# A convolution's sums on GpSimd, fewer weight tiles used whole, and the layer norm placed behind the convolution

## The chip, the cores and the metric

The kernel runs on 1 core of one Trainium2 chip. The metric is the device time of one execution in microseconds. One core has TensorE (PE, with its weight loads as PEld), VectorE (DVE), ScalarE (ACT), GpSimd (POOL) and SyncE (SP), each with its own queue, in which instructions are taken in program order; between engines they wait on semaphores.

## What is computed

Two blocks over 256 positions of 1024 channels, in float32. The first block has two layers, each a gated feed-forward, a mixer with short convolutions and a state-space part, a second feed-forward and a gated projection. The change lies in the second block, in its mixer:

```python
def conformer_conv(glu_in, conv_w, conv_b, ln_g, ln_b, w_conv_out):
    a, gate = jnp.split(glu_in, 2, axis=-1)
    v = a * jax.nn.sigmoid(gate)
    rhs = conv_w.astype(v.dtype)[:, None, :]
    v = lax.conv_general_dilated(v, rhs, window_strides=(1,), padding=[(CONV_K - 1, 0)],
                                 dimension_numbers=('NWC', 'WIO', 'NWC'),
                                 feature_group_count=CONV_WIDTH) + conv_b
    v = layernorm(v, ln_g, ln_b)
    v = jax.nn.silu(v)
    return v @ w_conv_out
...
h = rmsnorm_2(x, norm_mix_pre[l])
proj = h @ w_in[l]
u_pool, u_glu, g_a, g_b = jnp.split(proj, ...)
branch_a = pool_mixer(u_pool, pool_w[l], pool_scale[l], w_pool_out[l])
branch_b = conformer_conv(u_glu, conv_w[l], conv_b[l], conv_ln_g[l], conv_ln_b[l], w_conv_out[l])
merged = jax.nn.sigmoid(g_a) * branch_a + jax.nn.sigmoid(g_b) * branch_b
x = x + rmsnorm_2(merged @ w_o[l], norm_mix_post[l])
```

The convolution is causal and goes channel by channel, with 31 taps over 512 channels. The pool branch takes trailing means of 512 channels, a small product per group, and a projection. A feed-forward with a squared ReLU follows.

## The kernel before

Channels lie on the 128 partitions, the 256 positions along the free dimension. All weights lie in one stream of 4948 tiles of 128x128 in the order of their use. They come in pieces of 8 tiles through four buffers (`raw`). For most pieces ACT rounds the piece into `whi` (line 324) and DVE takes the difference into `wlo` (line 327), through a ring of five pairs; activations are split the same way (`split`, line 401). A tile then is three matmuls: hi by hi, hi by lo, lo by hi (line 366). The pieces between `WHOLE[0]` and `WHOLE[1]` are left as they are, and their tiles are multiplied in full float32 with an operand that isn't split (`Whole`, line 1369; `mm3`, line 375); the trace shows such a tile as two records. Here these are the last 104 tiles of `w_in_2`: 13 of the second block's 16 gate units.

A unit is 128 output channels: it takes a PSUM bank and multiplies its tiles, and a small routine then works off the bank. The order of instructions on each engine is made at build time by a small planner (`Flow`): routines run as generators, each operation adds an estimated cost to its engine's clock, and whichever routine is due next issues next. So the text of the program sets the order only in part; the costs set the rest.

The second block (`second`, line 978) first makes `xf`, the normed input that isn't split, and then works through `w_in_2` in this order: four pairs of units for the gated linear unit (`glu_part`), four for the pool branch (`pooled`), 16 for the two gates (`gate`), the first `NSPLIT` = 3 of them with split weights. A gate on split weights is multiplied by the norm's row on DVE first; one on whole weights is not, since `xf` has the row in it. Beside these units runs the convolution. The accumulator `cacc` (4 groups of 128 channels) starts with tap 30 and the bias on ACT (`conv_start`). For the other 30 taps there are two ways: ACT scales the shifted input into one of three product buffers (`conv_products`, ring `pr`) and DVE adds that product, 128x1024, to `cacc`; or DVE does a fused multiply-add for each of the four groups (`conv_sums`). `conv_sums` adds a product when one is ready and otherwise takes a tap from the other end.

When all units of `w_in_2` are issued, `layer_norm` is started: it waits for the sum (`cvdone`), takes a column sum on TensorE with a matrix of ones, subtracts the mean, squares, takes a second column sum, and makes the norm's row; `ln_out` then gives the four operands of `w_conv_out_2`. Beside it TensorE does `pool_w_2` (4 tiles) and `w_pool_out_2` (32 tiles); `w_conv_out_2` (32 tiles) follows.

In the profile `x` is the tile whose parts are `xf`, `cacc` and the product buffers, `sga` the gates, `cv` and `vv` scratch of the pool branch. Lines 237, 244, 257 and 266 are those of the helpers for a matmul, a two-operand DVE instruction, a fused DVE instruction and an activation.

Of the kernel before, what the change touches and what calls it, by code (L numbers as in the profile page):

```python
# [17 lines left out]
P = 128  # L18
T = 256
D = 1024  # L20
ND = D // P
# [5 lines left out]
EPS = 1e-6  # L27
# [5 lines left out]
SC_B, SC_C, SC_X, MZ, XBC, GA, GM = 0, 8, 16, 24, 40, 64, 72  # L33

NTILES = 4948
NWHOLE = 104
WHOLE_END = NTILES - (4 + 32 + 32 + 64 + 256 + 256)
WHOLE = (WHOLE_END - NWHOLE, WHOLE_END)
S = 8
# [39 lines left out]
class Event:  # L79
    def __init__(self, on=False):  # L80
        self.on, self.waiting = on, []


class Flow:
# [7 lines left out]

    def __init__(self):
        self.now, self.queue, self.count = 0.0, [], 0
        self.free = dict(pe=0.0, act=0.0, dve=0.0, dma=0.0)

    def spawn(self, gen, delay=0.0):
        heapq.heappush(self.queue, (self.now + delay, self.count, gen))
# [95 lines left out]
class Build:  # L194
# [783 lines left out]
    def second(self, sp, ss):  # L978
        nc = self.nc
        X = self.big.tile([P, 24, T], F32, name="x2", tag="X")  # L980
        xf = X[:, 0:8, :]
        cacc = X[:, 8:12, :]
        pr = Ring(self.flow, [X[:, 12:16, :], X[:, 16:20, :], X[:, 20:24, :]])
        glu = self.big.tile([P, 4, PAD + T], F32, name="glu", tag="ya")
        nc.vector.memset(glu[:, :, :PAD], 0.0)
        gluev = [Event() for _ in range(4)]
        xfo = Whole(xf)
        rb, r1b = (yield from self.rows.get()), (yield from self.rows.get())
# [39 lines left out]

        NSPLIT = 2 * ND - NWHOLE // ND
        cw = lambda n, k: self.v("conv_w_2", None, n * 31 + k)  # L1030
        shifted = lambda n, k: glu[:, n, k:k + T]
        taps = list(range(30))
        made, cvdone, cvinit = [], Event(), [Event() for _ in range(4)]

        def conv_start(n):
            yield gluev[n]
            yield self.act(cacc[:, n, :], shifted(n, 30), AF.Identity, scale=cw(n, 30), bias=self.v("conv_b_2", None, n))
            self.fire(cvinit[n])

        def conv_products():  # L1040

            for e in cvinit:
                yield e
            while len(taps) > 1:
                k = taps.pop(0)
                p = yield from pr.get()
                for n in range(4):
                    yield self.act(p[:, n, :], shifted(n, k), scale=cw(n, k))
                made.append(p)
            made.append(None)  # L1050

        def conv_sums():

            for n in range(4):
                yield cvinit[n]
            while taps or not made or made[0] is not None:
                if made and made[0] is not None:
                    p = made.pop(0)
                    yield self.add(cacc, cacc, p)
                    pr.put(p)  # L1060
                elif taps:
                    k = taps.pop()
                    for n in range(4):
                        yield self.stt(cacc[:, n, :], shifted(n, k), cw(n, k), cacc[:, n, :])
                else:
                    yield 0.2
            self.fire(cvdone)

        bs = yield from self.heads_of([(W, 0, 4), (W, 0, 8), (W, 0, 5), (W, 0, 9)], sp, ND)
        for n in range(4):  # L1070
# [5 lines left out]
            self.spawn(glu_part(n, ba, bg))  # L1076
            self.spawn(conv_start(n))
        self.spawn(conv_products())
        self.spawn(conv_sums())


        pm = Operand(self.big.tile([P, 4, 2 * T], F32R, name="pm", tag="V0"))
# [19 lines left out]
            yield from self.split(pm, n, pd)  # L1102
            self.vv.put(pd)

        sga = self.big.tile([P, 2 * ND, T], F32, name="sga", tag="V1")
        sgev = [Event() for _ in range(2 * ND)]

        def gate(n, b):
# [25 lines left out]


        px = yield from self.new_op()
        pc = Operand(px.tile[:, 4:, :])

        def layer_norm():
            yield cvdone  # L1140
            self.chains += 1
            b = yield from self.banks.get()
            for n in range(4):
                w = self.mm(b[:, :T], self.ones, cacc[:, n, :], n == 0, n == 3, cost=0.43)
            yield w
            mu = yield from self.rows.get()
            yield self.act(mu, b[:, :T], scale=1.0 / 512)
            self.banks.put(b)
            yield self.sub(cacc, cacc, mu.unsqueeze(1).to_broadcast([P, 4, T]))
            self.rows.put(mu)  # L1150
            p = yield from pr.get()
            yield self.act(p, cacc, AF.Square)
            yield self.add(p[:, 0:2, :], p[:, 0:2, :], p[:, 2:4, :])
            s = yield from self.new_sum(0)
            yield self.add(s["acc"], p[:, 0, :], p[:, 1, :])
            pr.put(p)
            self.fire(s["ev"])
            c, rl = self.small[18][:, :2], self.small[19][:, :2]
            yield from self.colsum(s, EPS, 512, c)
            if sgev[-1].on:  # L1160
                self.act(self.small[5], self.ones[:, :8], AF.Silu)
            yield from self.rsqrt(rl, c)
            rlb = yield from self.rows.get()
            yield from self.bcast([(rlb, 1.0)], rl)
            self.chains -= 1
            row = Shared(self.rows, rlb, 4)
            for n in range(4):
                self.spawn(ln_out(n, row))
                yield 0.4

        def ln_out(n, row):
            t = yield from self.t.get()
            yield self.mul(t, cacc[:, n, :], row.item)
            row.put()
            yield self.act(t, t, AF.Silu, scale=self.v("conv_ln_g_2", None, n), bias=self.v("conv_ln_b_2", None, n))
            yield from self.split(pc, n, t)
            self.t.put(t)

        self.spawn(layer_norm())

        def mixed(n, b):
            yield from self.split_scaled(px, n, b[:, :T], self.v("pool_scale_2", None, n))
# [2 lines left out]
        for n in range(4):  # L1185
            b = yield from self.banks.get()
# [11 lines left out]
        for n in range(ND):  # L1198
            b = yield from self.unit("w_pool_out_2", 0, n, px, 4)
# [3 lines left out]
        def merge(n, b):  # L1203
            yield sgev[ND + n]
            yield bev[n]
            u = yield from self.vv.get()
            yield self.mul(u, b[:, :T], sga[:, ND + n, :])
            self.banks.put(b)
            yield self.add(u, u, sga[:, n, :])
            yield from self.split(mg, n, u)  # L1210
            self.vv.put(u)

        for n in range(ND):
            b = yield from self.unit("w_conv_out_2", 0, n, pc, 4)
            self.spawn(merge(n, b))
        self.drop(px)
        for e in sgev + xfo.ev + [cvdone]:
# [3 lines left out]
        acc = yield from self.new_sum()  # L1221
# [7 lines left out]
        for n in range(ND):  # L1229
            b = bs[n] if n < 4 else (yield from self.unit("w_o_2", 0, n, mg, ND))  # L1230
# [19 lines left out]
        row = Shared(self.rows, rb, ND)  # L1250
# [29 lines left out]
        for j in range(NF2):  # L1280
            b = bs[j] if j < H else (yield from self.unit("w_up_2", 0, j, nsp, ND))
# [6 lines left out]
        row = self.big.tile([P, D], F32, name="gain", tag="xd0")  # L1288
# [42 lines left out]
        c, r = self.small[8][:, :2], self.small[9][:, :2]  # L1331
# [115 lines left out]
```

## Time and profile before

| | |
|---|---|
| median of 3 runs | 1822.45 us (1811.29 to 1824.0) |
| profiled execution | 1822.13 us |
| span of that execution | 1820.3 us |
| granted TensorE clock, mean | 0.993 |
| second block's convolution beside the gates | about 1500 to 1565 us of the span |
| layer norm to the first w_conv_out tile | 1566.5 to 1585.0 us |

The profile is one execution, seen by the hardware profiler. Times in its views are microseconds from the start of the span. A group of instructions gives the line, engine, operation, `out<-in` with tile names, and shapes, then busy time and the mean duration of one in ns, then the engine's idle time ahead of the group and what ended it. Neighbours on DVE and ACT overlap a little at their ends, so the distance of their starts is shorter than a duration.

### The profile page before, as it was taken

How to read it: one execution, taken by the hardware profiler on the slowest of the kernel's cores; microseconds unless marked ns; L12 is line 12 of the kernel's file. 1: busy time of each engine (PE TensorE's matmuls, PEld its weight loads, DVE VectorE, ACT ScalarE, POOL GpSimd, SP SyncE). 2: the span in 40 equal slices, each digit the busy share in tenths (PEclk: the TensorE clock that was granted, in tenths of full speed). 3: DMA queues.
4: the chain of work that ended last, by engine and by line, in shares of the span. 5: the costliest groups of instructions: out<-in, count | busy, mean ns of one | idle time of the engine just before them, and what ended most of it. 6: DMA issues, size and time to landing. Idle time of an engine off the chain costs nothing.

```text
span 1820.3 us, 36518 instructions
## 1 busy us (share of the span) xinstructions
PE 1789.6 (98%) x14900; PEld 1749.2 (96%) x14900; DVE 1318.0 (72%) x2236; ACT 1050.9 (58%) x1707; POOL 10.5 (1%) x22
## 2 busy tenths in 40 slices
PE   8999999999999999999999999999999999989997
PEld 7999999999999999999999999999999999889986
DVE  6666789887676666866678988767666689877643
ACT  5444579664555544654457966455554478656542
POOL 0000000000000000000000000000000000000000
PEclk9999999999999999999999999999999999989999
DMA  7666576655666666566657656466666653546552
GB/s 254 192 186 188 169 244 197 199 196 160 201 194 191 192 196 195 176 198 196 195 172 248 196 198 196 161 194 198 203 194 195 195 176 123 183 140 207 187 195 76
DMA packets 92696, 343.83 MB, mean 189 GB/s; under 512 B 10448, under 2 KB 10960, under 8 KB 91376
## 3 DMA queue, kind: packets, MB, share of 16 engines
q1 hardware_dynamic: 90720, 327.25, 57.4%
q0 software_dynamic: 1520, 13.73, 2.1%
q8 instruction: 116, 1.90, 0.4%
q10 hardware_dynamic: 288, 0.52, 0.1%
q14 instruction: 52, 0.43, 0.1%
HBM read 340.31 MB, written 1.15 MB: 188 GB/s over the span
## 4 chain that ended last, share of the span: by engine, by line
PE 91%; DVE 4%; ACT 2%; DMA 2%; issue 1%; SPq 0%; DVEq 0%; ACTq 0%
PE bank L237 90%; DMA raw<-in_w 1%; DVE wlo L244 1%; PE side L237 1%; ACT L266 1%; ACT whi L266 0%; PE bank L734 0%; DMA h<-in_x 0%; DVE cv L257 0%; DVE small L257 0%; DVE hs L257 0%; DVE acc L244 0%; DVE t L244 0%; DVE vv L257 0%; DVE hs L244 0%
## 5 line engine op out<-in xcount | busy, mean ns | idle before, releaser
L237 PE MATMUL bank<-hs,whi 128*128 128x256 f32 x6928 | 1215.0, 280 | 12.4 <-ACT whi L266 7.9
L237 PEld LDWEIGHTS bank<-hs,whi 128*128 128x128 f32 x6928 | 1055.0, 189 | 19.6 <-ACT whi L266 8.2
L244 DVE TENSOR_TENSOR wlo<-raw,whi 128x1024 fp32r<-128x1024 f32 (+1 forms) x602 | 733.0, 1220 | 378.9 <-ACT whi L266 377.5
L266 ACT ACTIVATE whi<-raw 128x1024 fp32r<-128x1024 f32 (+1 forms) x602 | 635.3, 1058 | 637.4 <-issue 320.1
L237 PE MATMUL bank<-hs,wlo 128*128 128x256 f32 x3464 | 965.7, 279 | 1.9 <-DVE wlo L244 1.8
L237 PEld LDWEIGHTS bank<-hs,wlo 128*128 128x128 f32 x3464 | 655.5, 189 | 2.8 <-DVE wlo L244 2.7
L237 PE MATMUL bank<-V,whi 128*128 128x256 f32 x1920 | 329.0, 277 | 0.0
L237 PEld LDWEIGHTS bank<-V,whi 128*128 128x128 f32 x1920 | 290.4, 188 | 0.0
L237 PE MATMUL bank<-V,wlo 128*128 128x256 f32 x960 | 265.8, 277 | 0.0
L237 PEld LDWEIGHTS bank<-V,wlo 128*128 128x128 f32 x960 | 180.2, 188 | 0.0
L237 PE MATMUL bank<-whi,V 128*128 128x512 f32 x256 | 79.8, 392 | 0.0
L244 DVE TENSOR_TENSOR t<-bank,row 128x256 f32<-128x256 f32 x159 | 64.4, 417 | 17.2 <-PE bank L237 11.1
L257 DVE SCALAR_TENSOR_TENSOR cv<-bank,vec,cv 128x253 f32<-128x253 f32 (+2 forms) x144 | 63.6, 474 | 3.8 <-ACT cv L266 3.2
L244 DVE TENSOR_TENSOR vv<-bank,t 128x256 f32<-128x256 f32 x152 | 62.6, 418 | 3.2 <-ACT t L266 2.9
L244 DVE TENSOR_TENSOR V<-vv,V 128x256 fp32r<-128x256 f32 x152 | 62.5, 420 | 1.5 <-ACT V L266 1.2
L266 ACT ACTIVATE V<-vv 128x256 fp32r<-128x256 f32 x152 | 60.1, 403 | 2.6 <-DVE vv L257 1.6
L237 PEld LDWEIGHTS bank<-whi,V 128*128 128x128 f32 x256 | 48.1, 188 | 10.7
L237 PE MATMUL bank<-wlo,V 128*128 128x512 f32 x128 | 50.1, 392 | 0.0
L266 ACT ACTIVATE dec<-dec,tb 128x256 f32<-128x256 f32 (+1 forms) x128 | 49.5, 445 | 0.1
L244 DVE TENSOR_TENSOR acc<-acc,sq 128x256 f32<-128x256 f32 x101 | 42.4, 420 | 8.6 <-ACT sq L266 8.0
L266 ACT ACT_TABLE_LOAD x37 | 47.5, 1283 | 1.3 <-PEq L1442 0.7
L266 ACT ACTIVATE hs<-h,vec 128x256 fp32r<-128x256 f32 x80 | 38.4, 498 | 11.9 <-DMA h<-in_x 7.1
(152 smaller groups left out, 1113.4 us busy)
## 6 DMA issues: line engine op xcount, KB each, us to landing
raw<-in_w SPq DMA_DIRECT2D x613, 512.0 KB, 4.3
dec<-cum_d POOLq DMA_DIRECT2D x8, 1536.0 KB, 10.0
extra<-in_w SPq DMA_DIRECT2D x4, 512.0 KB, 8.6
xt<-in_xt SPq DMA_DIRECT2D x1, 1024.0 KB, 11.5
h<-in_x SPq DMA_DIRECT2D x1, 512.0 KB, 8.6
praw<-in_p POOLq DMA_DIRECT2D x2, 256.0 KB, 4.5
gain<-in_row POOLq DMA_DIRECT2D x1, 512.0 KB, 4.7
out<-o SPq DMA_DIRECT2D x2, 256.0 KB, 2.7
```

The costliest lines, as they stand in the source:

```text
L237: self.nc.tensor.matmul(ps, w, x, start=start, stop=stop, **k)
L244: self.nc.vector.tensor_tensor(out, a, b, op=op)
L257: self.nc.vector.scalar_tensor_tensor(out, a, s, b, op0=op0, op1=op1)
L266: self.nc.scalar.activation(out=out, in_=a, func=func, **k)
```

## The change

The number of whole tiles becomes 40, so that 64 tiles that were whole (8 pieces) are now split, and 11 of the 16 gate units use split weights. A new accumulator `pacc`, 4 x 256 columns behind the gates in `sga`'s tile, takes the first tap's product; a new routine `conv_pool` adds later products to it on GpSimd. DVE adds a product only if two are waiting or no taps are left, and takes multiply-adds otherwise; at the end it adds `pacc` to `cacc`. `layer_norm` is started ahead of the pool and gate units and no longer behind them, so that its work is issued as soon as the planner has the convolution done; its first column sum uses the `side` bank, and its outputs wait until their operand's tile is had (`pcev`).

```diff
-NWHOLE = 104
+NWHOLE = 40
...
-        self.free = dict(pe=0.0, act=0.0, dve=0.0, dma=0.0)
+        self.free = dict(pe=0.0, act=0.0, dve=0.0, pool=0.0, dma=0.0)
...
+        sga = self.big.tile([P, 2 * ND + 4, T], F32, name="sga", tag="V1")
+        pacc = sga[:, 2 * ND:, :]
...
+            first = True
             while len(taps) > 1:
                 k = taps.pop(0)
-                p = yield from pr.get()
+                p = pacc if first else (yield from pr.get())
                 for n in range(4):
                     yield self.act(p[:, n, :], shifted(n, k), scale=cw(n, k))
-                made.append(p)
+                if not first:
+                    made.append(p)
+                first = False
             made.append(None)
+
+        def conv_pool():
+
+            while not made or made[0] is not None:
+                if made:
+                    p = made.pop(0)
+                    nc.gpsimd.tensor_tensor(pacc, pacc, p, op=ALU.add)
+                    yield self.flow.use("pool", 2.5)
+                    pr.put(p)
+                else:
+                    yield 0.2
+            self.fire(pldone)
...
-                if made and made[0] is not None:
+                if made and made[0] is not None and (len(made) > 1 or not taps):
                     p = made.pop(0)
                     yield self.add(cacc, cacc, p)
                     pr.put(p)
...
+            yield pldone
+            yield self.add(cacc, cacc, pacc)
             self.fire(cvdone)
...
+        self.spawn(conv_pool())
         self.spawn(conv_sums())
...
         def layer_norm():
             yield cvdone
             self.chains += 1
-            b = yield from self.banks.get()
+            b = yield from self.side.get()
...
+            yield pcev
             for n in range(4):
                 self.spawn(ln_out(n, row))
                 yield 0.4
...
         px = yield from self.new_op()
+        pc.append(Operand(px.tile[:, 4:, :]))
+        self.fire(pcev)
```

How the order moves on three engines. First GpSimd's queue from the second layer's mixer to the end, before; `dec`, `praw` and `gain` are loads that it issues, the last product is the output's:

```order
L699 DMA dec<-cum_d 128x3072 [waits DVE_49,DMASW0_49,PE_49,Activation_49]
L922 DMA praw<-in_p 128x512 [waits DMASW5_49,DVE_49,Activation_49]
L1289 DMA gain<-in_row 128x1024 [waits DMASW3_49,DVE_49]
L1302 TENSOR_TENSOR o<-junk,gain 128x512 [waits DMASW4_49,DMAHW4_49,DVE_49,Activation_49]
L1302 TENSOR_TENSOR o<-junk,gain 128x512 [waits Activation_49]
```

and after:

```order
L699 DMA dec<-cum_d 128x3072 [waits DVE_49,DMASW0_49,PE_49,Activation_49]
L922 DMA praw<-in_p 128x512 [waits DMASW5_49,DVE_49,Activation_49]
L1062 TENSOR_TENSOR sga<-sga,x_16346 128x1024 [waits DVE_49,DMASW2_49,PE_49,Activation_49]
L1062 TENSOR_TENSOR sga<-sga,x_16346 128x1024 [waits Activation_49,Pool_49] x14
L1314 DMA gain<-in_row 128x1024 [waits DMASW3_49]
L1327 TENSOR_TENSOR o<-junk,gain 128x512 [waits DMASW4_49,DMAHW4_49,DVE_49,Activation_49]
L1327 TENSOR_TENSOR o<-junk,gain 128x512 [waits Activation_49]
```

15 sums into `pacc` stand between the loads, each waiting for a product of ACT and for the sum before it, and the load of the gain stands behind them.

Second, VectorE at the end of the convolution, before. `x2` from `glu` is a multiply-add of a tap, `x2` from `x2` the add of a product, `h` the residual's scaling, `hs1` the pool branch's operand, `x2` with `row0` the norm's first subtraction:

```order
L244 TENSOR_TENSOR x2_16346<-x2_16346 128x1024 [waits DVE_49,Activation_49] x2
L257 SCALAR_TENSOR_TENSOR x2_16346<-glu_16347,vec_129,x2_16346 128x256 [waits DVE_49]
L257 SCALAR_TENSOR_TENSOR x2_16346<-glu_16347,vec_129,x2_16346 128x256
L244 TENSOR_TENSOR wlo2_83<-raw3_77,whi2_82 128x1024 [waits DMAHW3_49,Activation_49]
L257 SCALAR_TENSOR_TENSOR x2_16346<-glu_16347,vec_129,x2_16346 128x256
L244 TENSOR_TENSOR h_130<-h_130,row2_116 128x512
L257 SCALAR_TENSOR_TENSOR x2_16346<-glu_16347,vec_129,x2_16346 128x256
L244 TENSOR_TENSOR h_130<-h_130,row2_116 128x512 x2
L244 TENSOR_TENSOR wlo3_85<-raw2_76,whi3_84 128x1024 [waits DMAHW4_49,Activation_49]
L244 TENSOR_TENSOR h_130<-h_130,row2_116 128x512
L257 SCALAR_TENSOR_TENSOR hs1_95<-bank3_69,vec_129,hs1_95 128x256 [waits Activation_49]
L244 TENSOR_TENSOR x2_16346<-x2_16346,row0_114 128x1024 [waits Activation_49]
```

and after:

```order
L257 SCALAR_TENSOR_TENSOR x2_16346<-glu_16347,vec_129,x2_16346 128x256 x2
L257 SCALAR_TENSOR_TENSOR x2_16346<-glu_16347,vec_129,x2_16346 128x256 [waits DVE_49] x9
L244 TENSOR_TENSOR wlo0_79<-raw3_77,whi0_78 128x1024 [waits DMAHW3_49,Activation_49]
L257 SCALAR_TENSOR_TENSOR x2_16346<-glu_16347,vec_129,x2_16346 128x256 [waits DVE_49] x3
L244 TENSOR_TENSOR x2_16346<-x2_16346 128x1024 [waits DVE_49,Activation_49]
L244 TENSOR_TENSOR wlo1_81<-raw2_76,whi1_80 128x1024 [waits DMAHW4_49,Activation_49]
L244 TENSOR_TENSOR x2_16346<-x2_16346,sga_16349 128x1024 [waits DVE_49,Pool_49]
L257 SCALAR_TENSOR_TENSOR hs1_95<-bank2_68,vec_129,hs1_95 128x256 [waits Activation_49]
L257 SCALAR_TENSOR_TENSOR hs1_95<-bank0_66,vec_129,hs1_95 128x256 [waits Activation_49]
L257 SCALAR_TENSOR_TENSOR hs1_95<-bank5_71,vec_129,hs1_95 128x256 [waits Activation_49]
L257 SCALAR_TENSOR_TENSOR hs1_95<-bank4_70,vec_129,hs1_95 128x256 [waits Activation_49]
L244 TENSOR_TENSOR x2_16346<-x2_16346,row0_114 128x1024 [waits DVE_49,Activation_49]
```

The adds of products have become multiply-adds (one add is left), the scaling of `h` has moved behind, and a final add waits for GpSimd with all four `hs1` rows behind it.

Third, TensorE from the last gate to the pool branch's projection, before; `pm` is the operand of `pool_w_2`, the products with `ones` are the norm's column sum:

```order
L237 MATMUL bank1_67<-x2_16346,raw0_74 128x256 x7
L237 MATMUL bank3_69<-pm_16632,whi2_82 128x256 [waits Activation_49]
L237 MATMUL bank3_69<-pm_16632,whi2_82 128x256
L237 MATMUL bank3_69<-pm_16632,wlo2_83 128x256 [waits DVE_49]
L237 MATMUL bank0_66<-x2_16346,ones_132 128x256 x2
L237 MATMUL bank0_66<-x2_16346,ones_132 128x256 [waits DVE_49] x2
L237 MATMUL bank5_71<-pm_16632,whi2_82 128x256 x2
L237 MATMUL bank5_71<-pm_16632,wlo2_83 128x256
```

and after:

```order
L237 MATMUL bank5_71<-pm_16633,whi0_78 128x256 x2
L237 MATMUL bank5_71<-pm_16633,wlo0_79 128x256
L237 MATMUL bank4_70<-pm_16633,whi0_78 128x256 x2
L237 MATMUL bank4_70<-pm_16633,wlo0_79 128x256
L237 MATMUL side_73<-x2_16346,ones_132 128x256 [waits DVE_49]
L237 MATMUL side_73<-x2_16346,ones_132 128x256 x3
L237 MATMUL bank6_72<-hs1_95,whi0_78 128x256 [waits Activation_49]
L237 MATMUL bank6_72<-hs1_95,whi0_78 128x256 [waits DVE_49]
```

The column sum has moved from between the first and second of the four `pool_w_2` units to behind the fourth; in both versions it stands ahead of `w_pool_out_2` (the products with `hs1`).

More of the change, by code (lines that the diff above doesn't have):

```diff
@@ L1032, in second @@
         taps = list(range(30))
-        made, cvdone, cvinit = [], Event(), [Event() for _ in range(4)]
+        made, cvdone, cvinit, pldone = [], Event(), [Event() for _ in range(4)], Event()
         def conv_start(n):
@@ L1078, in second, with layer_norm, ln_out @@
         self.spawn(conv_products())
+        self.spawn(conv_pool())
         self.spawn(conv_sums())
+        pc, pcev = [], Event()
+        def layer_norm():
+            yield cvdone
+            self.chains += 1
+            b = yield from self.side.get()
+            for n in range(4):
+                w = self.mm(b[:, :T], self.ones, cacc[:, n, :], n == 0, n == 3, cost=0.43)
+            yield w
+            mu = yield from self.rows.get()
+            yield self.act(mu, b[:, :T], scale=1.0 / 512)
+            self.side.put(b)
+            yield self.sub(cacc, cacc, mu.unsqueeze(1).to_broadcast([P, 4, T]))
+            self.rows.put(mu)
+            p = yield from pr.get()
+            yield self.act(p, cacc, AF.Square)
+            yield self.add(p[:, 0:2, :], p[:, 0:2, :], p[:, 2:4, :])
+            s = yield from self.new_sum(0)
+            yield self.add(s["acc"], p[:, 0, :], p[:, 1, :])
+            pr.put(p)
+            self.fire(s["ev"])
+            c, rl = self.small[18][:, :2], self.small[19][:, :2]
+            yield from self.colsum(s, EPS, 512, c)
+            if sgev[-1].on:
+                self.act(self.small[5], self.ones[:, :8], AF.Silu)
+            yield from self.rsqrt(rl, c)
+            rlb = yield from self.rows.get()
+            yield from self.bcast([(rlb, 1.0)], rl)
+            self.chains -= 1
+            row = Shared(self.rows, rlb, 4)
+            yield pcev
+            for n in range(4):
+                self.spawn(ln_out(n, row))
+                yield 0.4
+        def ln_out(n, row):
+            t = yield from self.t.get()
+            yield self.mul(t, cacc[:, n, :], row.item)
+            row.put()
+            yield self.act(t, t, AF.Silu, scale=self.v("conv_ln_g_2", None, n), bias=self.v("conv_ln_b_2", None, n))
+            yield from self.split(pc[0], n, t)
+            self.t.put(t)
+        self.spawn(layer_norm())
         pm = Operand(self.big.tile([P, 4, 2 * T], F32R, name="pm", tag="V0"))
@@ L1103, in pooled @@
             self.vv.put(pd)
-        sga = self.big.tile([P, 2 * ND, T], F32, name="sga", tag="V1")
         sgev = [Event() for _ in range(2 * ND)]
@@ L1136, in second @@
         px = yield from self.new_op()
[L1137 to L1141, printed above, removed]
-            b = yield from self.banks.get()
[L1143 to L1179, printed above, removed]
+        pc.append(Operand(px.tile[:, 4:, :]))
+        self.fire(pcev)
         def mixed(n, b):
@@ L1213, in second @@
         for n in range(ND):
-            b = yield from self.unit("w_conv_out_2", 0, n, pc, 4)
+            b = yield from self.unit("w_conv_out_2", 0, n, pc[0], 4)
             self.spawn(merge(n, b))
```

## The prediction

> **What bounds the kernel now.** I read the page's first part, then the chain of waits, then the stage of the convolution as a window, its groups of instructions, and the order of time.
>
> ```profile
> span 1820.3 us, 36518 instructions
> PE 1789.6 (98%) x14900; PEld 1749.2 (96%) x14900; DVE 1318.0 (72%) x2236; ACT 1050.9 (58%) x1707; POOL 10.5 (1%) x22
> ...
> PE 91%; DVE 4%; ACT 2%; DMA 2%; issue 1%; SPq 0%; DVEq 0%; ACTq 0%
> ```
>
> TensorE is busy 98% of the span and carries 91% of the chain, so the kernel is matmul-bound over its length. GpSimd is all but unused. That is an average; the change touches one stage, the second block's input projection with the convolution beside it.
>
> ```profile
> 1506.40:1564.50 58.10, 58.10 (x334) 52.93 (x333) 55.37 (x110) 45.22 (x110) 0.00 (x0) 1.00 0.42 142
> ```
>
> The columns are the stretch, its length, then busy time of PE, weight load, DVE, ACT, POOL, then clock and DMA. PE never stops, yet DVE is busy 55.37 of 58.10 us. DVE is a second bound 3 us behind the first. Its groups there:
>
> ```profile
> L244 DVE TENSOR_TENSOR x<-x 128x1024 f32<-128x1024 f32 x22 | 26.8, 1219 | 1.2 <-ACT x L266 0.7
> L257 DVE SCALAR_TENSOR_TENSOR x<-glu,vec,x 128x256 f32<-128x256 f32 x32 | 14.6, 478 | 0.1
> L244 DVE TENSOR_TENSOR wlo<-raw,whi 128x1024 fp32r<-128x1024 f32 (+1 forms) x4 | 4.1, 1016 | 0.6 <-ACT whi L266 0.6
> L244 DVE TENSOR_TENSOR h<-h,row 128x512 f32<-128x512 f32 x3 | 2.0, 683 | 0.0
> L244 DVE TENSOR_TENSOR cv<-bank,row 128x256 f32<-128x256 f32 x4 | 1.7, 418 | 0.0
> L244 DVE TENSOR_TENSOR t<-bank,row 128x256 f32<-128x256 f32 x3 | 1.3, 423 | 0.6 <-PE bank L237 0.6
> ```
>
> 22 taps are summed as 128x1024 adds, 8 taps as 32 fused multiply-adds. Only the last two groups read a PSUM bank; nearly everything else reads two SBUF tensors. Next, what follows the stage:
>
> ```profile
> L237 PE MATMUL bank<-x,raw x208: 377/379/382, 1520.8 to 1565.9; 128*128 128x256 f32 x104
> L237 PE MATMUL bank<-x,ones x8: 378/379/379, 1566.5 to 1568.0; 128*128 128x256 f32 x8
> ...
> 1584.97 32.83 PE bank L237 x287
> ```
>
> The 104 whole tiles (two records each) run from 1520.8 to 1565.9. The layer norm's first matmul follows at 1566.5, and w_conv_out starts at 1584.97, from the chain: 18.5 us of layer norm with the pool products beside it.
>
> **The change, part by part.**
>
> *64 tiles more are split.* One split tile is three matmuls; consecutive tiles start 0.34 us apart:
>
> ```profile
> 1497.31 0.39 PE L237 MATMUL bank<-hs,whi 128*128 128x256 f32 x2
> 1497.53 0.28 PE L237 MATMUL bank<-hs,wlo 128*128 128x256 f32 x1
> 1497.65 0.39 PE L237 MATMUL bank<-hs,whi 128*128 128x256 f32 x2
> ```
>
> A whole tile takes (1565.9 - 1520.8) / 103.5 = 0.436 us. PE saves 64 x 0.096 = 6.1 us, if nothing makes it wait. In return 8 pieces need a rounding on ACT and a subtraction on DVE, and 8 more gates a multiplication by the row on DVE.
>
> *Work on DVE.* Starts of neighbours give the price of each in a full queue:
>
> ```profile
> 1510.22 1.21 DVE L244 TENSOR_TENSOR x<-x 128x1024 f32<-128x1024 f32 x1
> 1511.35 0.47 DVE L257 SCALAR_TENSOR_TENSOR x<-h,vec,row 128x256 f32<-128x256 f32 x1
> 1511.75 1.22 DVE L244 TENSOR_TENSOR x<-x 128x1024 f32<-128x1024 f32 x1
> 1512.88 0.41 DVE L244 TENSOR_TENSOR cv<-bank,row 128x256 f32<-128x256 f32 x1
> 1513.22 1.21 DVE L244 TENSOR_TENSOR x<-x 128x1024 f32<-128x1024 f32 x1
> ```
>
> An add or a piece's subtraction costs 1.13, a fused multiply-add 0.40, a product with a bank 0.34. By the program's order DVE now has 13 taps as 52 multiply-adds (20 more), 2 adds (20 fewer), 9 more pieces ahead of the final add (8, and one of the next stage that stood behind it), 8 more bank products, and 3 halves of h moved behind. From 55.4: - 22.6 + 8.0 + 10.2 + 2.7 - 1.8 = 51.9 us. So DVE gives up 15 adds and gets nearly all of it back in other work.
>
> *Work on GpSimd.* 15 adds of 128x1024. Before, the only arithmetic of that kind on it stands at the very end:
>
> ```profile
> 1810.00 1.26 POOL L1302 TENSOR_TENSOR o<-junk,gain 128x512 f32<-128x512 f32 x1 [532.91 <-DVE small L262]
> 1810.05 1.24 DVE L257 SCALAR_TENSOR_TENSOR small<-small,small 128x1 f32<-128x1 f32 x1
> ...
> 1810.00 2.48 POOL L1302 TENSOR_TENSOR o<-junk,gain 128x512 f32<-128x512 f32 x2 [532.91 <-DVE small L262]
> 1810.05 2.46 DVE L257 SCALAR_TENSOR_TENSOR small<-small,small 128x1 f32<-128x1 f32 x2
> ...
> 1494.61 0.54 DVE L257 SCALAR_TENSOR_TENSOR small<-small,small 128x1 f32<-128x1 f32 x3
> ...
> L1442 POOL MEMSET const-float32-0.0<- 128x1 f32 x1 | 0.1, 99 | 0.2 <-issue 0.2
> ```
>
> 128x512 takes 1.24 to 1.26 us. Of 128x1024 the trace has none: twice that is 2.52 us at most, and less the 0.10 of the smallest POOL row, as if all of that were start-up, 2.38 at least. 15 cost 35.7 to 37.8 us; I take 37.
>
> The same rows decide the case. A DVE multiply-add on one column costs 0.54 / 3 = 0.18 us at 1494. At 1810.05 the same instruction takes 1.24 us: it ends when the POOL add does, and the second one ends with the second POOL add, 2.46 us for two. DVE read two SBUF tensors, POOL read two, and DVE stood still. I take it that this holds for the convolution's rows, which have the same form with more columns.
>
> The Trainium skill, page "SBUF — State Buffer", section "Who interferes with whom", states it as a rule: a DVE instruction with two SBUF inputs and a GpSimd instruction that reads SBUF exclude each other for a whole instruction, whichever comes first; DVE instructions with one SBUF input pass. The trace agrees with the first half (1.24 against 0.18 us); no row here shows the second. By that second half all 15 bank products would slip through, and the sum below would be about 1845 rather than 1848.
>
> *The sum.* DVE's work and POOL's do not lie side by side but one behind the other, except where DVE has a bank product at its head (11 t and 4 cv at 0.34: 0 to 5.1 us hidden).
>
> ```profile
> 1506.37 0.48 DVE L257 SCALAR_TENSOR_TENSOR x<-glu,vec,x 128x256 f32<-128x256 f32 x1
> ...
> 1508.35 1.21 DVE L244 TENSOR_TENSOR wlo<-raw,whi 128x1024 fp32r<-128x1024 f32 x1
> ```
>
> From 1506.4, the first multiply-add, the final add on DVE ends at 1506.4 + 51.9 + (35.7 to 37.8) - (0 to 5.1) = 1588.9 to 1596.1; I take 1592. In before that sum was ready before 1566.5. The subtraction at 1508.35 is done some 8 us before the first split tiles that need it run out at 1520.8; that lead is eaten after three or four POOL adds, and then TensorE waits for wlo, so its 6.1 us are lost in waits. The final add waits for POOL, and behind it in DVE's queue stand the pool branch's hs rows, for which w_pool_out waits; on PE the layer norm's matmul stands ahead of w_pool_out. From there the path is before's: 18.5 us to w_conv_out, now at 1610.5 instead of 1584.97, 25.5 us late. What follows is unchanged. The profiled execution took 1822.13 (span 1820.3 and 1.8 around it), 0.3 below the median 1822.45: 1822.1 + 25.5 = 1847.6, so 1848. From the two ends, with 2 us off the norm's path at best and 6 us of slow clock at worst: 1842 to 1858.
>
> *What costs nothing.*
>
> ```profile
> L266 ACT ACTIVATE x<-glu,vec 128x256 f32<-128x256 f32 x86 | 36.4, 496 | 0.4 <-DVE x L244 0.4
> ...
> 1509.09 4.89 ACT L266 ACTIVATE x<-glu,vec 128x256 f32<-128x256 f32 x12
> ...
> 1276.56 0.53 POOL L1289 DMA_DIRECT2D gain<-in_row  x1 [50.12 <-DVE small L257]
> ```
>
> ACT makes 20 products fewer (4.89 / 12 = 0.41 each, 8.2 us) and 8 roundings more; with 45.22 of 58.10 us busy it stays behind DVE's work, and if it were late, POOL would idle and DVE run. It now waits for POOL to free one of three product buffers, with roundings queued behind that wait; POOL's 15 adds end before DVE's list does, so this only decides who waits first. The gain's DMA, issued at 1276.56 in before, falls behind the 15 adds in POOL's queue, to about 1590; it is needed past 1800.
>
> **The rivals.**
>
> *GpSimd runs beside DVE.* If the 1.24 us were a matter of one-column instructions, DVE's 51.9 us end at 1558, PE ends the gates at 1559.8, the norm's matmul comes about 1561, w_conv_out at 1579.5: 5.5 us early, 1817, on the other side. For it speaks only that no row shows a long DVE instruction beside POOL. It decides once less than about 8 of POOL's 37 us reach DVE: then the final add still ends before 1566.5.
>
> *Half of it.* DVE is held only for part of each POOL add, some 18 us in all: the final add at 1574, w_conv_out at 1592.5, 7.5 us late, 1830. Against it: the DVE rows at 1810 ended with the POOL adds, not midway.
>
> *The sum, and a slow clock on top.* A TensorE that waits loses its clock:
>
> ```profile
> 1618.00:1620.00 2.00, 0.71 (x4) 0.52 (x4) 1.17 (x3) 0.57 (x2) 0.00 (x0) 1.00 0.52 158
> 1620.00:1622.00 2.00, 0.00 (x0) 0.00 (x0) 1.77 (x11) 0.00 (x0) 0.00 (x0) 0.69 0.66 225
> ...
> 1630.00:1632.00 2.00, 2.00 (x15) 2.00 (x14) 2.00 (x6) 0.55 (x2) 0.00 (x0) 0.75 0.00 0
> 1632.00:1634.00 2.00, 2.00 (x20) 2.00 (x19) 0.59 (x3) 1.56 (x3) 0.00 (x0) 1.00 0.04 8
> ```
>
> After a wait of 3 us the granted clock falls, and comes back about 10 us later. If it is at half through the 32 tiles of w_pool_out (10.9 us) and the norm's sums, those take some 26 us instead of 13 and outlast the 18.5: 7.5 us more, 1855. For it: long waits of PE are what the forecast means. Against: the waits come in pieces, between bursts of 2.7 us for eight tiles.
>
> **How the numbers follow.** The sum 0.60, the sum with a slow clock 0.13, half 0.12, beside 0.15. The time is that of the likeliest, 1848, its own range 1842 to 1858. For 8 in 10 the range reaches down past the half case and up past the slow clock: 1826 to 1862, which leaves out the 0.15 and some of the tails. One per cent is about what a measurement of this kernel can tell from no change: 1804.2 and 1840.7 are the borders. Slower by over 1%: 0.13 and most of the 0.60 (its low end is near the border), 0.64. Faster by over 1% would take more than the 6.1 us at stake: 0.02. Within 1%: 0.34.
>
> **What would show it.** Right: POOL with 15 adds of about 2.4 to 2.6 us, the DVE group x<-glu,vec,x with a mean well above 478 ns, PE waiting for DVE wlo between 1520 and 1590, the norm's first matmul near 1592 and w_conv_out near 1610. Wrong: multiply-adds still at 478 ns while POOL adds run, or that matmul before 1566. A granted clock of 0.5 about 1590 to 1600 would mark the third rival. POOL adds much longer than 2.5 us would mean that POOL waits for DVE instead; the sum stays.

## The result and the profile after

| | before | after |
|---|---|---|
| median of 4 runs | 1822.95 us (1811.29 to 1824.0) | 1848.47 us (1847.64 to 1849.97) |
| profiled execution, its span | 1822.13, 1820.3 us | 1849.27, 1847.1 us |
| layer norm's first matmul | 1566.5 us | 1588.4 us |
| first tile of w_conv_out | 1584.97 us | 1608.55 us |

The ratio is 1.0151, 95% interval 1.0129 to 1.0174: about 1.5% slower. Two executions of the runs below, one of the kernel before (6664 us) and one with the sums alone (4639 us), are left out of the ratios, though not of the medians. The profile's first part, after:

```profile
span 1847.1 us, 36664 instructions
PE 1795.6 (97%) x14964; PEld 1754.8 (95%) x14964; DVE 1342.2 (73%) x2252; ACT 1050.8 (57%) x1695; POOL 49.9 (3%) x37
```

The shares hardly move: 97% for 98 on TensorE, 3% for 1 on GpSimd. The stage shows what the average hides. Its window from the first multiply-add to the final add, then two parts of it, with the columns as in the prediction (length, busy time of PE, weight load, DVE, ACT, POOL, clock, DMA):

```profile
1505.00:1588.30 83.30, 63.31 (x417) 58.84 (x415) 78.90 (x125) 45.93 (x102) 39.89 (x16) 0.88 0.32 105
1505.00:1560.00 55.00, 45.69 (x343) 43.69 (x341) 55.00 (x79) 33.11 (x71) 27.35 (x11) 0.94 0.36 114
1570.00:1588.30 18.30, 17.61 (x74) 15.15 (x74) 13.90 (x29) 9.34 (x22) 6.01 (x4) 0.82 0.39 133
```

Before, PE filled its window; now it is idle for 20.0 of 83.3 us. DVE shows 55.00 busy of 55.00 up to 1560, but much of that is not work, as its groups from 1505.0 to 1588.4 show:

```profile
L257 DVE SCALAR_TENSOR_TENSOR x<-glu,vec,x 128x256 f32<-128x256 f32 x52 | 38.5, 760 | 0.0
L244 DVE TENSOR_TENSOR wlo<-raw,whi 128x1024 fp32r<-128x1024 f32 (+1 forms) x13 | 17.7, 1363 | 4.0 <-ACT whi L266 4.0
L244 DVE TENSOR_TENSOR cv<-cv 128x256 f32<-128x256 f32 x10 | 8.3, 827 | 0.0
L257 DVE SCALAR_TENSOR_TENSOR small<-small,small 128x1 f32<-128x1 f32 (+1 forms) x9 | 5.6, 651 | 0.0
L244 DVE TENSOR_TENSOR t<-bank,row 128x256 f32<-128x256 f32 x11 | 4.5, 412 | 0.0
```

The multiply-adds took 478 ns each before and take 760 now. Groups with two SBUF inputs whose rows met a GpSimd add are longer (cv 827 ns, 419 before); the one that reads a bank is not (412 ns, 423 before). One by one, first DVE and then POOL, in order of time (start, duration):

```profile
1510.46 2.63 DVE L257 SCALAR_TENSOR_TENSOR x<-glu,vec,x 128x256 f32<-128x256 f32 x1
1513.35 0.47 DVE L257 SCALAR_TENSOR_TENSOR x<-glu,vec,x 128x256 f32<-128x256 f32 x1
1513.74 2.63 DVE L244 TENSOR_TENSOR cv<-cv 128x256 f32<-128x256 f32 x1
...
1527.09 1.22 DVE L244 TENSOR_TENSOR wlo<-raw,whi 128x1024 fp32r<-128x1024 f32 x1
...
1547.69 0.41 DVE L244 TENSOR_TENSOR t<-bank,row 128x256 f32<-128x256 f32 x1
```

```profile
1510.34 2.48 POOL L1062 TENSOR_TENSOR sga<-sga,x 128x1024 f32<-128x1024 f32 x1 [285.30 <-ACT x L266]
1513.52 2.57 POOL L1062 TENSOR_TENSOR sga<-sga,x 128x1024 f32<-128x1024 f32 x1 [0.71 <-ACT x L266]
...
1526.97 3.94 POOL L1062 TENSOR_TENSOR sga<-sga,x 128x1024 f32<-128x1024 f32 x1 [3.67 <-ACT x L266]
...
1547.70 4.91 POOL L1062 TENSOR_TENSOR sga<-sga,x 128x1024 f32<-128x1024 f32 x2 [3.94 <-ACT x L266]
```

A multiply-add that starts 0.12 us after a POOL add ends at 1513.09; the add ended at 1512.82. The bank row at 1547.69 passes in 0.41 us while an add runs. At 1526.97 it is POOL that stands: the add beside wlo lasts 3.94 us, 1.4 to 1.5 more than the three adds ahead of it. So the hold goes both ways. The starts don't tell which of the two stands: at 1510.34 and at 1526.97 the add has the same lead of 0.12 us.

What TensorE waited for from 1500 to 1610 (total, times, longest), and the tile of the 15 adds (shortest, median, longest in ns):

```profile
PE side L237 <- DVE small L257: 11.9, 1, 11.9
PE bank L237 <- DVE wlo L244: 8.1, 5, 2.3
PE bank L237 <- ACT hs L266: 2.9, 2, 2.5
```

```profile
L1062 POOL TENSOR_TENSOR sga<-sga,x x15: 2359/2475/3938, 1510.3 to 1580.1; 128x1024 f32<-128x1024 f32 x15
```

The longest wait is not the forecast one for wlo. It is the broadcast of the residual's row, which needs eleven small DVE operations and stands in the middle of the whole tiles on PE.

### The profile page after: what moved, and what is told of

Its sections match the earlier page's. It is cut to its first block, busy times and chain, and to the rows that moved or that the text cites. A ratio compares the mean times of both kernels' runs of the same rounds, so it can differ in the third digit from the quotient of the medians.

```text
span 1847.1 us, 36664 instructions
## 1 busy us (share of the span) xinstructions
PE 1795.6 (97%) x14964; PEld 1754.8 (95%) x14964; DVE 1342.2 (73%) x2252; ACT 1050.8 (57%) x1695; POOL 49.9 (3%) x37
## 4 chain that ended last, share of the span: by engine, by line
PE 87%; DVE 8%; ACT 2%; DMA 2%; issue 2%; SPq 0%; DVEq 0%; ACTq 0%
PE bank L237 85%; DVE wlo L244 2%; DVE x L257 1%; DMA raw<-in_w 1%; PE side L237 1%; DVE cv L257 1%; DVE small L257 1%; ACT whi L266 1%; DVE cv L244 0%; DVE t L244 0%; ACT L266 0%; PE bank L734 0%; ACT dec L266 0%; DMA h<-in_x 0%; DVE vv L244 0%
## 5 line engine op out<-in xcount | busy, mean ns | idle before, releaser
L237 PE MATMUL bank<-hs,whi 128*128 128x256 f32 x7056 | 1242.9, 281 | 12.8 <-ACT whi L266 6.9
L237 PEld LDWEIGHTS bank<-hs,whi 128*128 128x128 f32 x7056 | 1079.0, 190 | 20.6 <-ACT whi L266 7.2
L244 DVE TENSOR_TENSOR wlo<-raw,whi 128x1024 fp32r<-128x1024 f32 x610 | 745.5, 1225 | 383.0 <-ACT whi L266 381.3
L266 ACT ACTIVATE whi<-raw 128x1024 fp32r<-128x1024 f32 x610 | 643.8, 1058 | 641.6 <-issue 323.2
L237 PE MATMUL bank<-hs,wlo 128*128 128x256 f32 x3528 | 986.1, 279 | 10.2 <-DVE wlo L244 10.2
L237 PEld LDWEIGHTS bank<-hs,wlo 128*128 128x128 f32 x3528 | 668.1, 189 | 12.4 <-DVE wlo L244 12.3
L1062 POOL TENSOR_TENSOR sga<-sga,x 128x1024 f32<-128x1024 f32 x15 | 39.4, 2625 | 318.0 <-ACT x L266 317.6
```

The lines of the kernel that those rows point to most:

```text
L237: self.nc.tensor.matmul(ps, w, x, start=start, stop=stop, **k)
L244: self.nc.vector.tensor_tensor(out, a, b, op=op)
L266: self.nc.scalar.activation(out=out, in_=a, func=func, **k)
L1062: nc.gpsimd.tensor_tensor(pacc, pacc, p, op=ALU.add)
```

## The experiments

Three theories were open. The *hold* theory: GpSimd's adds stop DVE's rows with two SBUF inputs, and everything else follows. The *order* theory: 64 more split tiles, the layer norm amid the gates, or the place of the residual's row cost the time, and the hold matters little. The *write* theory: any GpSimd traffic in SBUF does it. The before kernel ran beside each group of runs, at 1821.54, 1822.11 and 1822.07 us. For each run the median and the ratio to it with the 95% interval are given.

### The same order without the sums' size

One column of each product is added on GpSimd, and the rest of these products is left out of the sum; the order on every engine is that of the changed kernel.

```diff
-                    nc.gpsimd.tensor_tensor(pacc, pacc, p, op=ALU.add)
+                    nc.gpsimd.tensor_tensor(pacc[:, 0, :1], pacc[:, 0, :1], p[:, 0, :1], op=ALU.add)
```

> The changed kernel with the same order on every engine and the same waits, but each of GpSimd's 15 adds covers one column instead of 1024 (the products that GpSimd sums are left out of the result). Theory (the two engines exclude each other for the length of a GpSimd add): the hold goes, DVE's 51.9 us end near 1558, w_conv_out starts near 1579 and the time is about 1817, 25 to 35 us below the changed kernel; the multiply-adds stay at 478 ns. Rival (the new order costs it: more pieces on DVE, the layer norm and the residual's row placed elsewhere, POOL's adds merely stand by): about 1848, unchanged.

1818.59 us, 0.9973 (0.9958 to 0.9989). The group of multiply-adds in the stretch 1505 to 1562, and the tile of the norm's first matmul:

```profile
L257 DVE SCALAR_TENSOR_TENSOR x<-glu,vec,x 128x256 f32<-128x256 f32 x52 | 23.8, 478 | 0.0
```

```profile
L237 PE MATMUL side<-x,ones x8: 379/379/483, 1561.2 to 1562.9; 128*128 128x256 f32 x8
```

With the adds' size gone, 52 multiply-adds take 478 ns again, the norm begins at 1561.2, and the kernel is some 3 us faster than before. The rest of the change gains a little; the adds as such cost 1848.47 - 1818.59 = 30 us.

### The old order with adds beside it

Two runs keep every line of before and let GpSimd make 15 adds into scratch, of which nothing is used. In the first they have nothing to wait for:

```diff
...
+            nc.gpsimd.memset(pacc, 0.0)
+            for _ in range(15):
+                nc.gpsimd.tensor_tensor(pacc, pacc, pacc, op=ALU.add)
```

> The kernel before with its order, 104 whole tiles and its layer norm as they were; GpSimd alone gets 15 adds of 128x1024 on a scratch tile that nobody reads, in one burst as the convolution's products begin. Theory: DVE loses 15 x 2.45 = 36.8 us less two or three of its own bank products' time, and had 2.7 us to spare, so the layer norm begins about 32 us later and the time is about 1850 to 1857. Rival (the order costs it): 1822 as before, since no order has changed.

1840.91 us, 1.0097 (1.0079 to 1.0114), below what was expected. GpSimd's order of time tells why:

```profile
1441.37 33.56 POOL L1048 TENSOR_TENSOR sga<-sga 128x1024 f32<-128x1024 f32 x15
```

The burst ran one stage too early, where it held other rows (wlo 1875 ns for 1223 from 1441 to 1475). In the second run the first add reads the convolution's first product, which puts the burst in the right place:

```diff
...
+                if k == 0:
+                    nc.gpsimd.tensor_tensor(pacc, p, p, op=ALU.add)
+                    for _ in range(14):
+                        nc.gpsimd.tensor_tensor(pacc, pacc, pacc, op=ALU.add)
```

> The kernel before, its order and its 104 whole tiles, with 15 adds of 128x1024 on a scratch tile that nobody reads on GpSimd, the first waiting for the convolution's first product, so that they run beside the convolution and not ahead of it. Theory: DVE has under 3 us to spare there and only seven bank products that can pass, so of 15 x 2.45 = 37 us some 30 to 34 arrive at the layer norm: 1846 to 1856. Rival (the changed order costs it): 1822.

1846.45 us, 1.0115 (1.0083 to 1.0148). Its burst in GpSimd's order of time (the later 14 adds), and DVE's groups from 1505 to 1591:

```profile
1511.08 31.04 POOL L1055 TENSOR_TENSOR sga<-sga 128x1024 f32<-128x1024 f32 x14
```

```profile
L244 DVE TENSOR_TENSOR x<-x 128x1024 f32<-128x1024 f32 x22 | 31.6, 1434 | 1.8 <-ACT x L266 1.3
L257 DVE SCALAR_TENSOR_TENSOR x<-glu,vec,x 128x256 f32<-128x256 f32 x32 | 22.4, 722 | 0.1
L244 DVE TENSOR_TENSOR cv<-bank,row 128x256 f32<-128x256 f32 x4 | 1.6, 412 | 0.0
```

Adds that take nothing off DVE, in an order that did not change, cost 24 us. The multiply-adds go from 478 to 722 ns and the 128x1024 adds from 1219 to 1434, while the bank rows stay. The order theory can't give this.

### Which accesses hold

Half the columns; a copy with one input; a fill that only writes. All three keep the changed kernel's code otherwise and leave out some or all of GpSimd's sum.

```diff
-                    nc.gpsimd.tensor_tensor(pacc, pacc, p, op=ALU.add)
+                    nc.gpsimd.tensor_tensor(pacc[:, :2, :], pacc[:, :2, :], p[:, :2, :], op=ALU.add)
```

> The changed kernel with the same order and waits, GpSimd's 15 adds on 512 of the 1024 columns (half of the products that GpSimd sums are left out). Theory (DVE loses what GpSimd's adds last): the hold falls from about 37 to 15 x 1.25 = 19 us, the final add comes near 1570 instead of 1588, and the time lies between the one-column kernel's 1819 and the changed kernel's 1848, at 1825 to 1832. Rivals: below 1821 if DVE can take half of the hold for nothing, 1842 or more if the number of adds and not their length counts.

```diff
-                    nc.gpsimd.tensor_tensor(pacc, pacc, p, op=ALU.add)
+                    nc.gpsimd.tensor_copy(pacc, p)
```

> The changed kernel with the same order and waits, GpSimd's 15 adds replaced by copies of the product into the same tile (one input read, 1024 columns; the sum of the products is left out). Theory (a GpSimd instruction that reads SBUF excludes DVE's two-input rows for its length): the held rows last as long as a copy, about 1 to 1.3 us, 15 to 19 us in all, 1823 to 1832. Rival (only two inputs on both sides exclude each other): multiply-adds at 478 ns and about 1818.

```diff
-                    nc.gpsimd.tensor_tensor(pacc, pacc, p, op=ALU.add)
+                    nc.gpsimd.memset(pacc, 0.0)
```

> The changed kernel with GpSimd's 15 adds replaced by 15 fills of the same 128x1024 tile (the products that GpSimd sums are left out); same order and waits, but the instruction only writes. Theory (only a GpSimd instruction that reads SBUF excludes DVE's two-input rows): multiply-adds at 478 ns and about 1818, as with one column. Rival (any GpSimd access does): a fill of about 1 us each holds DVE 15 us and the time is 1824 to 1832.

| GpSimd's instruction | its length | multiply-add | median | ratio |
|---|---|---|---|---|
| add, one column | 0.35 us | 478 ns | 1818.59 | 0.9973 (0.9958 to 0.9989) |
| fill, 1024 columns | 0.96 us | 479 ns | 1818.86 | 0.9985 (0.9969 to 1.0) |
| copy, 1024 columns | 1.27 us | 591 ns | 1827.06 | 1.0022 (1.0003 to 1.004) |
| add, 512 columns | 1.54 us | 665 ns | 1824.74 | 1.0028 (1.0012 to 1.0045) |
| add, 1024 columns | 2.48 us | 760 ns | 1848.47 | 1.0151 (1.0129 to 1.0174) |

Lengths are medians of the 15. The multiply-adds are those of the profiled execution, which is not a typical one for two rows: 1820.45 us for the copy, near the lower end of its ten, and 1832.99 for the add of 512 columns, the highest of its ten. That add's median lies just below what was expected. For the copy and then the fill, the tile on POOL:

```profile
L1062 POOL COPY sga<-x x15: 1040/1272/2594, 1502.8 to 1553.4; 128x1024 f32<-128x1024 f32 x15
```

```profile
L1062 POOL MEMSET sga<- x15: 955/957/960, 1508.1 to 1522.3; 128x1024 f32 x15
```

and DVE's group, of the copy (1500 to 1562), of the fill, and of the add of 512 columns:

```profile
L257 DVE SCALAR_TENSOR_TENSOR x<-glu,vec,x 128x256 f32<-128x256 f32 x49 | 28.0, 591 | 0.0
```

```profile
L257 DVE SCALAR_TENSOR_TENSOR x<-glu,vec,x 128x256 f32<-128x256 f32 x52 | 23.9, 479 | 0.0
```

```profile
L257 DVE SCALAR_TENSOR_TENSOR x<-glu,vec,x 128x256 f32<-128x256 f32 x52 | 33.5, 665 | 0.0
```

The fills ran 14 us beside DVE and cost nothing, so writes don't hold: the write theory falls. A single input is enough: the copy, of the same 1024 columns, raises the multiply-adds to 591 ns. The fill also took every wait for products away, so it is a clean test of the hold but not of the schedule. The time does not go linearly with the hold, as the profiled executions show when each is set beside its own multiply-adds: 591 ns with 1820.45 us and the norm's first matmul at 1562.3, where one column has it at 1561.2; 665 ns with 1832.99 us and 1573.0; 760 ns with 1849.27 us and 1588.4. The executions of the half-sized adds lie in two clusters, 1822.6 to 1825.1 and 1830.9 to 1833.0, and the profile is of the upper one, so their median says little; why there are two is open.

### The accumulator in PSUM

If DVE's multiply-adds read one operand from a bank, they should pass. `cacc` is put in two banks; the sums are complete.

```diff
...
-                        yield self.stt(cacc[:, n, :], shifted(n, k), cw(n, k), cacc[:, n, :])
+                        yield self.stt(cg(n), shifted(n, k), cw(n, k), cg(n))
...
-            yield self.add(cacc, cacc, pacc)
+            for i in range(2):
+                yield self.add(cacc[:, 2 * i:2 * i + 2, :].rearrange("p a t -> p (a t)"), cps[i][:, :], pacc[:, 2 * i:2 * i + 2, :].rearrange("p a t -> p (a t)"))
```

> The changed kernel with the convolution's accumulator in two PSUM banks, so that DVE's multiply-adds read one SBUF tensor and one bank; GpSimd's 15 adds, the 40 whole tiles and the early layer norm stay. Theory (GpSimd's adds exclude only DVE instructions with two SBUF inputs): no multiply-add is held, their mean stays near 480 ns, and DVE is held only at the subtractions of pieces and the pool branch's sums; as such a row follows every one or two multiply-adds, some 10 us of the 37 are hidden and the time is 1832 to 1842. Rival (GpSimd's adds hold DVE whatever it reads): mean near 765 ns and about 1848.

1839.95 us, 1.0099 (1.0066 to 1.0132). DVE's groups from 1505 to 1583, then a piece of its order of time:

```profile
L257 DVE SCALAR_TENSOR_TENSOR bank<-glu,vec,bank 128x256 f32<-128x256 f32 x52 | 24.5, 481 | 0.2
L244 DVE TENSOR_TENSOR cv<-cv 128x256 f32<-128x256 f32 x10 | 10.5, 1052 | 0.0
L244 DVE TENSOR_TENSOR vv<-vv,cv 128x2 f32<-128x2 f32 (+3 forms) x4 | 6.3, 1580 | 0.0
```

```profile
1567.76 5.06 DVE L257 SCALAR_TENSOR_TENSOR bank<-glu,vec,bank 128x256 f32<-128x256 f32 x11
```

Eleven multiply-adds run in 5.06 us (0.46 each) while POOL adds are under way, from 1567.58 to 1570.06 and again from 1571.88. Yet only 8.5 us come back. The rows that still read two SBUF tensors now catch a part of what the multiply-adds caught: cv goes from 827 to 1052 ns, vv from 705 to 1580, 5.8 us for both. The accumulator also takes two banks from the units of TensorE; what that costs was not tried alone. DVE keeps an order, and the first held row stops all behind it.

### The parts of the change alone

Four runs take the change apart: tiles and early norm without GpSimd's sums; sums and early norm with 104 whole tiles; early norm alone; sums alone. With 104 whole tiles GpSimd makes 13 adds. The second edit is against the changed kernel, the others against the kernel before; the moved call stands ahead of the pool and gate units, with the side bank and `pcev` as in the change. Where the sums are on GpSimd, the rest of their code is that of the change too.

```diff
-NWHOLE = 104
+NWHOLE = 40
...
+        self.spawn(layer_norm())
```

> 40 whole tiles and the early layer norm as in the changed kernel, but GpSimd sums nothing: products are added on DVE as before. Theory: no hold, but DVE has 8 pieces and 8 products by the row more than before (11.8 us) in a stage that TensorE would end 6 us sooner, so DVE's list becomes the bound: 55.4 + 11.8 - 1.8 = 65.4 us from 1506.4 ends near 1573, w_conv_out near 1592, time 1826 to 1832. Rival (the order costs it): 1845 or more, since DVE has more work than in the changed kernel.

```diff
-NWHOLE = 40
+NWHOLE = 104
```

> The changed kernel with 104 whole tiles; by the planner GpSimd then takes 13 adds. Theory: DVE's list loses 8 pieces and 8 products by the row (51.9 - 11.8 = 40.1 us, 4 more multiply-adds), POOL holds 13 x 2.45 = 31.9 us: the final add near 1578, w_conv_out near 1597, time 1830 to 1837, still slower than before. Rival (the additional split tiles cost it, not POOL): 1820 to 1823.

```diff
...
+        self.spawn(layer_norm())
```

> The kernel before with nothing but the layer norm's new place: 104 whole tiles, sums on DVE. Theory: the norm's first matmul is issued where DVE ends the sums, within 2 us of before's 1566, and the time is 1819 to 1825. Rival (the early norm puts an in-order wait in TensorE's queue ahead of work it could do): 1830 or more.

```diff
...
+                if made:
+                    p = made.pop(0)
+                    nc.gpsimd.tensor_tensor(pacc, pacc, p, op=ALU.add)
+                    yield self.flow.use("pool", 2.5)
+                    pr.put(p)
```

> The kernel before with GpSimd's sums (13 adds) as the only part of the change: 104 whole tiles, the layer norm in its old place behind the gates. Theory (the early norm puts its column sum in TensorE's queue amid the gates, and with the hold TensorE waits there with 26 tiles behind it): without it TensorE goes on with the gates, the norm begins near 1575 and the time is 1828 to 1838, below the 1846 of the kernel with both. Rival (the hold alone gives the 1846, wherever the norm stands): 1843 to 1849.

| parts | median | ratio |
|---|---|---|
| early norm | 1820.17 | 0.9995 (0.9974 to 1.0016) |
| early norm, 40 whole tiles | 1838.97 | 1.0088 (1.0071 to 1.0104) |
| sums on GpSimd, norm in its old place | 1841.03 | 1.0103 (1.0086 to 1.012) |
| sums on GpSimd, early norm | 1845.86 | 1.0131 (1.0116 to 1.0146) |
| all three | 1848.47 | 1.0151 (1.0129 to 1.0174) |

Three of the four missed their ranges, only the early norm alone went as expected. Sums alone cost 19 us; the early norm adds 5 where DVE is late, and nothing where it isn't. With both, TensorE stands at the norm's column sum, with whole tiles behind it in its queue:

```profile
PE side L237 <- DVE x L244: 10.9, 1, 10.9
```

In the run with the sums alone it goes on with those tiles until the norm begins at 1577.8. With the sums and the early norm, 40 whole tiles and the two more adds that come with them add 3 us at most; the intervals of these two ratios overlap. The tiles without the sums cost 17 us, more than expected, and the window of that run shows why:

```profile
1504.30:1584.10 79.80, 68.90 (x513) 65.48 (x511) 76.19 (x137) 63.71 (x134) 0.00 (x0) 0.97 0.47 156
```

DVE has 76.19 us of its own work up to the last tap at 1584, with GpSimd idle, where 65.4 were expected: the split tiles' pieces and the next stage's come on top of all the convolution's sums. So the two parts need each other on paper: GpSimd is to free the DVE time that the split tiles take. In that run the planner also put w_pool_out (from 1562.0) ahead of the norm (from 1584.5), so that the norm's path had nothing beside it; how the excess divides between these two was not tried.

### The residual's row, moved

The longest wait, 11.9 us, was removed by starting the row behind the convolution:

```diff
+            yield cvdone
...
-            yield 30.0
```

> The changed kernel with the residual's row (square root on DVE, broadcast on TensorE) made after the convolution instead of in the middle of the gates, where TensorE waited 11.9 us for it. Theory (the shared port sets the end, TensorE's wait only stands in front of it): the final add comes at most 5 us earlier, 1842 to 1846. Rival (that in-order wait is what the change costs): 12 us earlier, about 1836.

1849.26 us, 1.0159 (1.0138 to 1.018): nothing gained, and above what was expected. TensorE's waits in that run, and the tile of the norm's first matmul:

```profile
PE bank L237 <- DVE wlo L244: 13.5, 6, 6.4
PE bank L237 <- ACT whi L266: 3.5, 1, 3.5
PE side L237 <- DVE x L244: 2.5, 1, 2.5
```

```profile
L237 PE MATMUL side<-x,ones x8: 631/631/792, 1586.6 to 1589.8; 128*128 128x256 f32 x8
```

The row's wait is gone, and the waits for wlo grow from 8.1 to 13.5 us. The norm starts 1.8 us sooner, with matmuls of 631 ns for 379. The wait that the table named first only stood in front of the real bound, which is the length of DVE's list.

## Why the prediction was right

**The hold.** The prediction took one-column rows at 1810 as evidence for rows of 256 columns. That step held: the multiply-adds beside POOL lasted 2.63 us, and the runs show it in the new order (30 us between one column and all) and in the old (24 us with scratch adds). Both rivals below the forecast, beside and half, fall with these; half had 18 us of hold, and 27 were felt. The Trainium skill, page "SBUF — State Buffer", section "Who interferes with whom", has the rule for it. Its second half, that DVE rows with one SBUF input pass, the prediction could not show; the traces here agree with it, by 0.41 us at 1547.69 and 481 ns with the accumulator in PSUM. That whichever comes first holds the other, as the prediction also has it, can't be read off the starts in these traces. The prediction's 1845 for all bank products passing goes with the lower end of POOL's time; with its 37 us the sum gives 1846.

**DVE's list and the sum.** Forecast: 51.9 us of work, 35.7 to 37.8 of hold, 0 to 5.1 hidden; the final add at 1592. Measured: 1588.3. The work was right: in the one-column run the same 125 rows keep DVE busy for 51.95 us up to the end of the final add, and here for 78.90, so DVE felt 27.0 us of hold. By groups, against the same groups of the one-column run: multiply-adds 38.5 - 23.8 = 14.7; wlo, its 12 whole pieces alone, 17.3 - 14.6 = 2.7; cv 8.3 - 4.2 = 4.1; the small rows 5.6 - 1.5 = 4.1; vv 4 x (0.705 - 0.165) = 2.2. That is 27.8, as neighbours overlap a little at their ends. GpSimd's adds lasted 39.4 us:

```profile
L1062 POOL TENSOR_TENSOR sga<-sga,x 128x1024 f32<-128x1024 f32 x15 | 39.4, 2625 | 318.0 <-ACT x L266 317.6
```

So some 12 us of them did not hold DVE. About 4.0 are POOL's own stand beside rows that had begun (39.4 - 15 x 2.36, the shortest add); 4.0 fell on a wait of DVE, from 1577.8 to 1581.7; the 4 or so that remain are for rows that pass, where the forecast had 0 to 5.1. The mis-sized term is the hold: 33.7 us net of what was hidden, by the forecast's 1592, and 27.0 measured, as the sum had no POOL add beside a DVE that waits. Two smaller errors stand against each other: DVE began at 1505.0 and not at 1506.4, and it was idle for 83.3 - 78.9 = 4.4 us, most of it for roundings on ACT, which the sum did not have (the one-column run has 4.3). - 1.4 - 6.7 + 4.4 = - 3.7 us.

**TensorE's loss.** Its 6.1 us were lost in waits, as forecast. But the waits for wlo make only 8.1 us; the 11.9 us for the residual's row were not named. The moved row shows that this did not change the end.

**The norm's path.** 18.5 us were taken from before; it took 1608.55 - 1588.4 = 20.2. The chain of waits on it, after:

```profile
1599.92 0.65 DVE wlo L244
...
1601.48 1.13 DVE wlo L244
...
1603.95 1.13 DVE wlo L244
...
1607.02 1.14 DVE wlo L244
```

Four subtractions of pieces stand on it, where before's chain has two:

```profile
1577.14 1.15 DVE wlo L244
...
1583.12 1.13 DVE wlo L244
```

Between the norm's first matmul and w_conv_out DVE makes six of them now and made five before; why two more stand on the chain was not tried.

**Behind it.** The prediction put nothing here and kept a slow clock for a rival. Windows of after (the clock is the last but two):

```profile
1612.00:1614.00 2.00, 2.00 (x11) 2.00 (x11) 1.64 (x4) 0.00 (x0) 0.00 (x0) 0.50 0.82 262
1614.00:1616.00 2.00, 2.00 (x18) 2.00 (x17) 0.53 (x2) 1.37 (x2) 0.00 (x0) 0.93 0.01 4
```

From 1608 to 1614 TensorE has a granted clock of 0.50 and starts 11 matmuls in 2 us; before, at 1.00, it starts 20 of w_conv_out's. The shift grows from 23.6 us at w_conv_out to 26.2 at the next column sum (1645.3 for 1619.1) and 26.8 at the end of the span, 3.2 more in all. A slow clock did come, about w_conv_out and not about w_pool_out where the rival had it (1.00 from 1588 to 1607), for less than half of the rival's 7.5 us. It came among the gates too, at 0.50 from 1540 to 1542, from 1547 to 1549, and up to 1576.

The terms against the forecast: final add 3.7 us sooner, norm's path 1.7 longer, behind it 3.2 longer. Their sum is +1.2, and the span's shift is 26.8 for 25.5. The close agreement rests in part on errors of opposite sign.

**What costs nothing.** The gain's DMA was issued at 1582.38, forecast 1590, and nothing waited for it. ACT was to stay behind DVE's work; but DVE waited 4.0 us for its roundings (the row of wlo above), where the one-column run has 1.9.

## What to carry to other kernels

Before giving GpSimd elementwise work on SBUF, count the rows with two SBUF inputs that VectorE must do meanwhile: here the 15 adds would have been 17 us on VectorE (15 x 1.13), and on GpSimd they made it stand for 27 of the 39 us that they lasted. A write-only fill, or VectorE rows that read a PSUM bank, do run beside GpSimd, but a single two-input row ahead of them in the queue passes the hold on. Don't take the longest wait in the table for the bound; remove it in a run of its own, as the residual's row here, before building on it.

## What the runs showed of the hardware that was not expected

- A GpSimd copy with one input holds VectorE too (multiply-adds 591 ns for 478), while a fill does not (479): it is GpSimd's reading that counts, as the same section of the Trainium skill says, and one input is enough for it.
- The hold goes both ways: a POOL add that started 0.12 us ahead of a long VectorE row took 3.94 us. In the run with the sums alone one started at 1561.07, amid 13 multiply-adds that ran back to back in 5.23 us from 1559.66, and took 6.03 us, the longest:

```profile
L1062 POOL TENSOR_TENSOR sga<-sga,x x13: 2338/2461/6032, 1510.4 to 1567.2; 128x1024 f32<-128x1024 f32 x13
```

- Short waits are enough for a slow clock: from 1526 to 1539 TensorE waited three times, 1.87 us at most, and the granted clock stood at 0.50 from 1540 to 1542; from 1598 to 1607 it was busy 6.17 of 9 us, with no single wait over 2.5 us, and the clock stood at 0.50 from 1608 to 1614. The prediction had seen it behind a wait of 3 us. The Trainium skill, page "TensorE: Matmul & The Clock Gate", section "The HAM clock gate", ties the lower clock to an idle window of about 3.4 us; no idle stretch of that length stands ahead of these two in this trace.
